# Conditioning vectors on VectorE, joined expert biases and gated rows, and a new seam between two blocks

## The chip, the cores and the metric

The kernel runs on one core of a Trainium2 chip, as one program. The metric is the time of one execution on the device in microseconds; the median of several runs counts. The core has TensorE (PE, with its weight loads listed as PEld), VectorE (DVE), ScalarE (ACT), GpSimd (POOL) and SyncE (SP), which here issues nearly all transfers from HBM.

## What is computed

256 tokens of 1024 channels pass through two blocks. Cut to what the change touches:

```python
def first_block(x, c, ctx, ...):
    mod_lat = split(silu(c) @ w_mod + b_mod, 6)        # 6 conditioning vectors of 1024
    h = rmsnorm(x, g) * (1 + mod_lat[1]) + mod_lat[0]
    x = x + mod_lat[2] * token_mixer(h, ...)           # latent attention + gated linear scan, w_in 1024x8256
    h = rmsnorm(x, g2) * (1 + mod_lat[4]) + mod_lat[3]
    x = x + mod_lat[5] * moe_ffn(h, ...)               # 32 experts, 4 per token
    return rmsnorm(x, final_norm_g)

def expert(xb, e):                                     # 1024 -> 2 x 1024 -> 1024
    gu = xb @ w_gate_up[e] + b_gate_up[e]
    act = swiglu(gu)
    return act @ w_down[e] + b_down[e]                 # weighted by the router, summed per token

def second_block(x, c_2, ...):
    mod = silu(c_2) @ w_ada + b_ada                    # 6 vectors of 1024
    h = modulate(rmsnorm(x, g_mix), sh1, sc1)
    ...                                                # recurrent mixer, then 32 small experts
    shf, scf = split(silu(c_2) @ w_ada_f + b_ada_f, 2) # 2 vectors, for the last norm
```

All is fp32. The weights make up nearly all of the 643 MB that are read.

## The kernel before

The program is recorded by a tile framework that places waits and orders each engine's instructions. Work comes in items of a queue: an `Item` has a part that asks for weights (`prep`) and a part that computes (`run`). `step()` prepares the first two items of the queue and runs the first; `fill(us)`, `need(item)` and `drain()` step through it, so that chains of other work (scan, attention) are interleaved with projections.

`wload` (L311) loads a weight tile of 128x2048 (1 MB) on SP's queue into the next of five slots; in MoE1 there are nine more (`w2x`, `w2`), 14 in all. A load whose slot is still read waits on SP, and every later load waits behind it. Projections (`tproj`) take a tile and split it into a high and a low part, a cast on ScalarE (L495) and a subtraction on VectorE (L496), both 128x1024, two for a tile of 1 MB; `mm3` (L508 to L510) makes three matmuls of 128x256 of each product, so a tile with eight row blocks is 48 matmuls.

**Block 1** (to 565 us) computes projections, the scan in four chains (0 to 3) and attention. Between the projections stand the "mods": one of 24 parts of 512 columns of a conditioning vector. `mod` loads two tiles of `wmod` or `wada`, and `modrow` makes 16 matmuls (L367) whose stationary operand holds the condition vector in one of 32 columns; VectorE adds the result into `rowall` (L369), one row per part. `fold_rows` and `mod_cols` turn the rows into columns when the block ends. 8 + 12 parts stand in block 1 (4 more for the first norm ahead of it), and the 4 of `wadaf` in block 2.

**MoE1** (577 to 1535 us) takes the 32 experts in turn, each of eight tiles `wgu` and four `wdn`, 12 MB. The rows of four experts, 64 each, are gathered at a time (L1278 to L1282). `expert1a` makes 64 matmuls gu (L1327) of 64 columns of tokens, in pairs for the two column halves, then the bias: four matmuls recorded, with a one-hot column as stationary operand against the table `brows` (L1402). `expert1b` transposes the activation, makes the 32 matmuls y (L1358), two of bias, and calls `combine`: yhi on ScalarE (L1236), ylo on VectorE (L1237), eight matmuls that scatter rows back to tokens (`co`, L1248), and per 128x512 piece of x a multiplication with the gate (L1253) and an addition (L1254) on VectorE. After expert 11 (`OVF`) the program looks whether some expert has more than 64 rows (L1292).

**The seam.** After the last expert x is normalised twice: once as the output of block 1 and once as the input of block 2. `xh` = x*gf (L1672), sums of squares (L1673, L1674), reciprocal roots (L431, L432); GpSimd multiplies x by r1 (L1681), VectorE xh by r2 (L1682); eight pairs of transposes (L1710); the results are scaled and shifted by VectorE (L1714) and ScalarE (L1715), and GpSimd makes the low part (L1716). Then the first projections of block 2 (`tproj` of `win2`) run, interleaved with a loop over low-rank products (`lora`, L1750 to L1760).

Of the kernel before, what the change touches and what calls it, by code (L numbers as in the profile page):

```python
# [18 lines left out]
EPS = 1e-6  # L19
# [4 lines left out]
MODS1 = [(1, j) for j in range(4, 12)] + [(2, j) for j in range(12)]  # L24
# [7 lines left out]
def _cols(a):  # L32
# [23 lines left out]
def _khalf(w):  # L56

    t = w.shape[1] // 512
    return np.ascontiguousarray(w.reshape(2, 4, 128, t, 512).transpose(3, 0, 2, 1, 4)).reshape(2 * t, 128, 2048)
# [62 lines left out]
def layout(i):  # L122
# [12 lines left out]
    d['wmod'] = _khalf(i['w_mod'][0])  # L135
    d['wmix'] = _ktile(i['w_mod'][0][:, :2048])
    d['wada'] = _khalf(i['w_ada_2'][0])
    d['wadaf'] = _khalf(i['w_ada_f_2'])
    mix = i['b_mod'][0][:2048].reshape(2, 4, 256).transpose(1, 0, 2).reshape(-1)
    d['bmods'] = np.ascontiguousarray(np.concatenate([mix, i['b_mod'][0][2048:], i['b_ada_2'][0], i['b_ada_f_2'], mix]).reshape(32, 512))  # L140
# [36 lines left out]
class Item:  # L177

    def __init__(self, prep, run):
        self.prep, self.run = prep, run  # L180
        self.ready = self.done = False
        self.gen = self.then = None
# [57 lines left out]
class Ker:  # L240
    def __init__(self, tc, d, out, dbg=None, stop=None, start=1):
        self.tc, self.nc, self.d, self.out = tc, tc.nc, d, out
        self.dbg = dbg or {}
        self.stop, self.start = stop, start
# [5 lines left out]
    def run(self):  # L250
        with ExitStack() as es:
# [10 lines left out]
            if self.start <= 1:  # L262
                with tc.tile_pool(name="t1late", bufs=1, side="right") as pl, tc.tile_pool(name="t1", bufs=1) as p:
                    self.early = lambda n: p.tile([128, 512], F32, name=n, tag="u", bufs=NU)
                    self.consts()
                    route = self.block1(p, pl, xtile)
            else:
                self.early = lambda n: self.cp.tile([128, 512], F32, name=n)
                self.consts()
                self.x1 = xtile("x").rearrange("p a (b n) -> p (a b n)", b=1).rearrange("p (b n) -> p b n", b=2)  # L270
                self.nc.sync.dma_start(self.x1, self.d['xin'])
                self.add(*(self.mod(2, j) for j in range(12)))
                self.drain()
                self.mod_cols((12, 10, self.mcol2[:, 0:40]))
# [4 lines left out]
            if self.start > 1:  # L279
                self.load_gf()  # L280
            if self.start <= 1:
                with tc.tile_pool(name="moe1", bufs=1, side="right", reuse_waits="tile") as p, tc.tile_pool(name="w2", bufs=NW2, reuse_waits="tile") as wp2, tc.tile_pool(name="w2x", bufs=NW2X, reuse_waits="tile") as wp3:
                    self.wq = own * NWR + [(wp3, "w")] * NW2X + [(wp2, "w")] * NW2
                    self.moe1(p, route, (wp2, "w"), (wp3, "w"))
# [29 lines left out]
    def consts(self):  # L314
# [23 lines left out]
        self.cpad2 = cp.tile([128, 504], F32, name="cpad2").rearrange("p (k n) -> p k n", k=8)  # L338
        nc.gpsimd.memset(self.cpad2, 0.0)
        nc.gpsimd.tensor_copy(self.cpad2[:, :, 31], cs[:, 16:24])  # L340
# [6 lines left out]
        self.mcol2 = cp.tile([128, 48], F32, name="mcol2")  # L347

# [4 lines left out]
    def msrc(self, which, j):  # L353
        src, r = {1: ('wmod', j), 2: ('wada', 12 + j), 3: ('wadaf', 24 + j)}[which]
        return [self.d[src][2 * j + a] for a in range(2)], r
# [15 lines left out]
    def mod(self, which, j):  # L371

        src, r = self.msrc(which, j)
        cpad = self.cpad1 if which == 1 else self.cpad2

        def run(ws):
            yield from self.modrow(cpad, r, [(0, lambda k: ws[k // 4][:, 512 * (k % 4):512 * (k % 4) + 512])])
        return Item(lambda: [self.wload(t) for t in src], run)
# [34 lines left out]
    def mod_cols(self, *todo):  # L413

        pt = self.fold_rows()
        for r, n, dst in todo:
            self.nc.vector.tensor_copy(dst.rearrange("p (j g) -> p g j", g=4), pt.rearrange("p (g r) -> p g r", g=4)[:, :, r:r + n])

    def bcast_rows(self, keys, dst, last=None):

        nc = self.nc
        for key, o in zip(keys, dst):
            ps = self.ps("bc")
            r = self.msrc(*key)[1]
            nc.tensor.matmul(ps, self.fold[:, r:r + 1].to_broadcast([128, 128]), self.rowall, start=True, stop=True)  # L425
            (last or nc.scalar.copy)(o, ps)
# [8 lines left out]
    def add(self, *items):  # L435
        self.q += items
        return items[-1]
# [99 lines left out]
    def block1(self, p, late, xtile):  # L537
# [255 lines left out]

        mods = [self.mod(*m) for m in MODS1]
        def mixed(items):
            out = []
            for it in items:
                out.append(it)
                if mods:
                    out.append(mods.pop(0))  # L800
# [66 lines left out]
        for pr in range(4):  # L867
# [4 lines left out]
            else:  # L872
                nxt = None
                lnexp()
                for i in range(3):
                    self.later(4 * i, lambda i=i: readout(i))
                self.add(*(tproj(win[28 + a], LAT, keep(qa, "qa", 3, qnorm)) for a in range(3)),
                         tproj(win[31], HS, keep(ckv, "ckv", 2, cnorm)), tproj(d['wrope'], HS, keep(kr, "kr"), nb=1, n=1024))
# [1352 lines left out]
```

## Time and profile before

| | us |
|---|---|
| median of 3 runs | 2112.69 (2109.07 to 2114.51) |
| the profiled execution, its own time | 2111.07 |
| its span in the trace | 2109.3 |

| engine | busy us | share of the span |
|---|---|---|
| PE | 1945.5 | 92% |
| PEld | 1114.6 | 53% |
| DVE | 896.0 | 42% |
| ACT | 511.6 | 24% |
| POOL | 63.3 | 3% |

The queue of weights (q1) takes 74.9% of the span of the 16 DMA engines; the mean rate is 306 GB/s. These shares are averages over stages with different limits, so the tables of windows, waits and single instructions are read stage by stage. Times in a timeline count from the span's start; a group of matmuls is listed with its start, its length and its count, and square brackets hold the idle time of the engine ahead of it and what ended that.

### The profile page before, as it was taken

The page shows a single profiled execution, that of the slowest core. Times are in us where ns is not written, and L with a number is a line of the kernel's source. Part 1 is how long each engine was busy: PE and PEld are TensorE (multiplying, and loading weights), DVE is VectorE, ACT ScalarE, POOL GpSimd, SP SyncE. Part 2 cuts the span into 40 slices and gives each one's busy share as a digit, 9 for nine tenths or more (in the row PEclk, how much of TensorE's full clock was granted, in tenths as well). Part 3 has the DMA queues.
Part 4 walks back from the last instruction along what each step waited for, and adds up shares of the span by engine and source line. Part 5 has one row for each costly group of instructions (what it writes and reads, how often), then busy time and mean ns, then how long its engine had stood idle before and what let it go on. Part 6 is the DMA issues. An engine that isn't in the chain of part 4 may idle for free. (4 is left out here: it accounts for less than half of the span.)

```text
span 2109.3 us, 30791 instructions
## 1 busy us (share of the span) xinstructions
PE 1945.5 (92%) x12860; PEld 1114.6 (53%) x12861; DVE 896.0 (42%) x1727; ACT 511.6 (24%) x893; POOL 63.3 (3%) x66
## 2 busy tenths in 40 slices
PE   5999999999899999989999999999969998899785
PEld 3888788877733333333333333333338997764331
DVE  5666754445423233332323333242378574421112
ACT  3433454344300001000000100000035543311011
POOL 0000000000000000000000000000032201000000
PEclk9999999999999999989999999999989999989897
DMA  9255636732699999979999999999873133289895
GB/s 362 81 219 201 227 126 258 278 111 80 262 415 427 411 427 416 427 295 407 426 427 427 426 427 427 426 427 427 365 292 124 62 121 103 114 370 420 360 425 226
DMA packets 95272, 646.11 MB, mean 306 GB/s; under 512 B 11668, under 2 KB 12692, under 8 KB 19220
## 3 DMA queue, kind: packets, MB, share of 16 engines
q1 hardware_dynamic: 93296, 642.79, 74.9%
q8 instruction: 104, 1.70, 0.3%
q10 hardware_dynamic: 1828, 1.26, 0.2%
q14 instruction: 44, 0.36, 0.0%
HBM read 642.96 MB, written 1.05 MB: 305 GB/s over the span
## 5 line engine op out<-in xcount | busy, mean ns | idle before, releaser
L1327 PE MATMUL gu<-w,gT 128*64 128x512 f32 x2048 | 481.2, 597 | 0.0
L1327 PEld LDWEIGHTS gu<-w,gT 128*64 128x64 f32 x2048 | 148.1, 137 | 278.1 <-issue 263.1
L1358 PE MATMUL y<-w,aT 128*64 128x512 f32 x1024 | 229.4, 601 | 0.4
L496 DVE TENSOR_TENSOR wsl<-w,wsh 128x1024 fp32r<-128x1024 f32 (+1 forms) x141 | 168.6, 1205 | 97.6 <-ACT wsh L495 97.3
L495 ACT CAST wsh<-w 128x1024 fp32r<-128x1024 f32 (+1 forms) x141 | 143.4, 1030 | 169.0 <-PE tp L509 97.4
L1337 DVE TENSOR_SCALAR act<-gu 128x256 f32<-128x256 f32 x64 | 27.2, 425 | 307.5 <-PE gu L1402 304.2
L1237 DVE SCALAR_TENSOR_TENSOR ylo<-y,sw,yhi 128x512 fp32r<-128x512 f32 x52 | 39.0, 751 | 264.5 <-ACT yhi L1236 264.0
L1358 PEld LDWEIGHTS y<-w,aT 128*64 128x64 f32 x1024 | 71.9, 139 | 148.6 <-issue 143.7
L508 PE MATMUL tp<-hs,wsh 128*128 128x256 f32 (+1 forms) x424 | 139.7, 329 | 0.0
L510 PE MATMUL tp<-hs,wsl 128*128 128x256 f32 (+1 forms) x424 | 134.3, 317 | 4.1 <-DVE wsl L496 4.1
L509 PE MATMUL tp<-hs,wsh 128*128 128x256 f32 (+1 forms) x424 | 133.6, 315 | 0.0
L1529 PE MATMUL ab<-w,gT 128*32 128x256 f32 (+1 forms) x1024 | 99.8, 415 | 17.4 <-DMA w<-in_w1e_dram 10.8
L1236 ACT ACTIVATE yhi<-y,sw 128x512 fp32r<-128x512 f32 x52 | 35.8, 688 | 300.9 <-PE y L1402 239.9
L1253 DVE TENSOR_TENSOR gated<-co,gtb 128x512 f32<-128x512 f32 x128 | 88.3, 690 | 34.6 <-PE co L1248 27.5
L1339 ACT ACTIVATE sge<-act 128x512 f32<-128x512 f32 x32 | 20.1, 630 | 331.3 <-DVE act L1337 331.3
L508 PEld LDWEIGHTS tp<-hs,wsh 128*128 128x128 f32 x424 | 81.7, 193 | 16.3 <-issue 4.9
L1254 DVE TENSOR_TENSOR x<-x,gated 128x512 f32<-128x512 f32 x128 | 88.3, 690 | 3.3
L510 PEld LDWEIGHTS tp<-hs,wsl 128*128 128x128 f32 x424 | 81.6, 193 | 9.9 <-DVE wsl L496 4.9
L508 PE MATMUL tp<-hi,wsh 128*128 128x256 f32 x288 | 85.4, 296 | 0.0
L509 PEld LDWEIGHTS tp<-hs,wsh 128*128 128x128 f32 x424 | 81.8, 193 | 4.5 <-issue 0.7
L1278 PE MATMUL ga<-oh,xhi 128*128 128x256 f32 x208 | 63.5, 333 | 21.9 <-PEq L1292 6.3
L509 PE MATMUL tp<-lo,wsh 128*128 128x256 f32 x288 | 81.7, 284 | 0.0
(576 smaller groups left out, 3099.9 us busy)
## 6 DMA issues: line engine op xcount, KB each, us to landing
w<-in_wgu_dram SPq DMA_DIRECT2D x256, 1024.0 KB, 15.3
w<-in_wdn_dram SPq DMA_DIRECT2D x128, 1024.0 KB, 15.6
w<-in_win_dram SPq DMA_DIRECT2D x50, 1024.0 KB, 5.9
w<-in_w3e_dram SPq DMA_DIRECT2D x32, 1024.0 KB, 14.7
w<-in_w1e_dram SPq DMA_DIRECT2D x32, 1024.0 KB, 11.9
w<-in_w2e_dram SPq DMA_DIRECT2D x32, 1024.0 KB, 15.9
w<-in_wada_dram SPq DMA_DIRECT2D x24, 1024.0 KB, 6.4
w<-in_wmod_dram SPq DMA_DIRECT2D x16, 1024.0 KB, 6.0
```

The costliest lines, as they stand in the source:

```text
L495: nc.scalar.copy(hi, src)
L496: nc.vector.tensor_sub(lo, src, hi.bitcast(F32))
L508: nc.tensor.matmul(out, a[0], b[0], start=first, stop=False)
L509: nc.tensor.matmul(out, a[0], b[1], start=False, stop=False)
L510: nc.tensor.matmul(out, a[1], b[0], start=False, stop=last)
L1237: nc.vector.scalar_tensor_tensor(lo, y, w, hi.bitcast(F32), op0=OP.mult, op1=OP.subtract)
L1253: nc.vector.tensor_mul(part, o[s], gate[:, cs])
L1254: nc.vector.tensor_add(x[:, b, cs], x[:, b, cs], part)
L1278: nc.tensor.matmul(ps[:, 256 * kk:256 * kk + 64 * n], xs[i][:, b, 128 * (k + kk):128 * (k + kk) + 128], ohv[b], start=(b + i == 0), stop=( ...
L1327: nc.tensor.matmul(gu[j][64 * s:64 * s + 64, :], g[:, k, c0:c0 + 64], w[:, 1024 * s + 512 * j:1024 * s + 512 * j + 512], start=(k == 0), s ...
L1358: nc.tensor.matmul(y[64 * s:64 * s + 64, :], aT[:, k % 4, k // 4, :], w[:, o:o + 512], start=(k == 0), stop=False)
L1529: nc.tensor.matmul(ps[m * j:m * j + m, 256 * i:256 * i + 256], g[:, k, c0 + m * j:c0 + m * j + m], w[j][:, k, :], start=(k == 0), stop=(k ...
```

## The change

It has four parts.

1. *Conditioning.* `w_mod`, `w_ada` and `w_ada_f` are stored by output column. A part of 512 columns is two "light" items of one tile each: VectorE multiplies 128x1024 weights with the condition vector, broadcast over partitions (`crow`: eight small matmuls and two copies, once for each of two vectors), and accumulates the sum into one column of `mcol` (L386 of the new kernel), twice, then adds the bias (L389). All 24 parts, the four of `wadaf` too, are 48 items of block 1: one behind each projection of the chains, two behind each g7 and wqb item. `step()` looks past light items until it has prepared two others.
2. *Joined biases.* In MoE1 the bias of gu is two matmuls and that of y one, each of 128 columns by 512, over both halves at once: the stationary operand is a block-diagonal one-hot (`brow`, 128x128, made by VectorE per expert), the other a table of high and low bias parts, loaded by 12 small DMAs and split once.
3. *Gated rows.* y is multiplied by the gate before it is split and combined (L1376), one 128x512 step per expert; `combine` only adds.
4. *Seam.* The down weights of expert 31 go into the nine MoE1 slots, and four tiles of `win2` are asked for behind them. xh is not scaled: the transposes become matmuls against diag(r2), into four PSUM tiles. x times r1 moves to ScalarE, behind the evacuations. The squares stand in a row with one reciprocal root.

```diff
+            def run(w):
+                yield 0
...
+                for i in range(2):
+                    wi = w[:, 1024 * i:1024 * i + 1024]
+                    n = 2 * a + i
+                    nc.vector.scalar_tensor_tensor(wi, wi, 1.0, c, op0=OP.mult, op1=OP.mult, accum_out=o[:, n:n + 1])
+                o = o[:, 2 * a:2 * a + 2]
+                b = VOFF[bias] + 4 * j + 2 * a
+                nc.vector.tensor_add(o, o, self.vec[:, b:b + 2])
+            return Item(lambda: self.wload(self.d[src][2 * j + a]), run, True)
+        return [half(0), half(1)]
...
     def step(self):
         it = self.q[0]
-        for i in self.q[:2]:
+        n = 0
+        for i in self.q:
             if not i.ready:
                 i.ready, i.w = True, i.prep()
+            n += not i.light
+            if n == 2:
+                break
...
-        lastg = [self.add(tproj(win[24 + i], LAT, g7)) for i in range(4)][-1]
+        lastg = [self.add(*mixed([tproj(win[24 + i], LAT, g7)], 2)) for i in range(4)][-1]
...
-            for s in range(2):
-                bias(gu[j][64 * s:64 * s + 64, :], 0, 1024 * s + 512 * j)
+            bias(gu[j], 0, 512 * j)
...
-        for s in range(2):
-            bias(y[64 * s:64 * s + 64, :], 1, 512 * s)
-        self.combine(p, x, y, oT, wv, gate)
+        bias(y, 1, 0)
+        part = p.tile([128, 512], F32, name="gated", tag="gated", bufs=1)
+        nc.vector.tensor_mul(part, y, gate)
+        self.combine(p, x, part, oT, wv)
...
+                return first.pop((e, j)) if (e, j) in first else fetch(e, j, ahead if e == 31 and j >= 8 else None)
...
+            rows = p.tile([128, 128], F32R, name="brow", tag="brow", bufs=2)
+            nc.vector.tensor_scalar(rows, blk, one, None, op0=OP.mult)
...
-        mods = [self.mod(3, j) for j in range(4)]
-        self.add(*mods)
-        for m in mods[:2]:
-            m.ready, m.w = True, m.prep()
-        ahead = [(self.wload(win2[2]),)]
+        ahead = {j: (self.wload(win2[j]),) for j in (2, 3, 0, 1)}
...
-            nc.gpsimd.tensor_mul(x[:, b, :], xh[b], r1[:, b:b + 1].to_broadcast([128, 1024]))
-            nc.vector.tensor_scalar(xh[b], xh[b], r2[:, b:b + 1], None, op0=OP.mult)
+            scaled = nc.vector.tensor_scalar(dg[:, 128 * b:128 * b + 128], self.ident, r2[:, b:b + 1], None, op0=OP.mult)
...
-                nc.tensor.transpose(pt[:, 128 * b:128 * b + 128], xh[b][:, 128 * k:128 * k + 128], self.ident)
+                nc.tensor.matmul(pt[k][:, 128 * b:128 * b + 128], xh[b][:, 128 * k:128 * k + 128], dg[:, 128 * b:128 * b + 128],
+                                 start=True, stop=True)
...
+        with tc.issue_after(evac.ins):
+            r1 = self.sm.tile([128, 2], F32, name="r1")
+            self.rstd_from(r1, st, 1024, self.eps)
+            for b in range(2):
+                nc.scalar.activation(x[:, b, :], xh[b], AF.Identity, scale=r1[:, b:b + 1])
```

VectorE in block 1, at the g7 items behind chain 3 (`wsl` is the low part of a projection's weights, `s` the scan's output). Before:

```order
L369 TENSOR_TENSOR rowall<-rowall,modps 128x512
L496 TENSOR_TENSOR wsl<-w,wsh 128x1024 x2
L864 TENSOR_TENSOR sg<-sg,tp 128x512
L865 TENSOR_TENSOR s_3680<-s_3680,sg 128x512
L369 TENSOR_TENSOR rowall<-rowall,modps 128x512
L496 TENSOR_TENSOR wsl<-w,wsh 128x1024 x9
L496 TENSOR_TENSOR wsl<-w,wsh 128x512
L496 TENSOR_TENSOR wsl<-w,wsh 128x1024
```

After:

```order
L878 TENSOR_TENSOR s_3575<-s_3575,sg 128x512
L507 TENSOR_TENSOR wsl<-w,wsh 128x1024 x2
L386 SCALAR_TENSOR_TENSOR w,mcol_97<-w,crow 128x1024 x2
L389 TENSOR_TENSOR mcol_97<-mcol_97,vec 128x2
L386 SCALAR_TENSOR_TENSOR w,mcol_97<-w,crow 128x1024 x2
L389 TENSOR_TENSOR mcol_97<-mcol_97,vec 128x2
L507 TENSOR_TENSOR wsl<-w,wsh 128x1024 x2
L386 SCALAR_TENSOR_TENSOR w,mcol_97<-w,crow 128x1024 x2
L389 TENSOR_TENSOR mcol_97<-mcol_97,vec 128x2
```

Between two projections' weight splits, where nothing or one addition stood, now stand four multiplications of 128x1024 and two additions.

PE in MoE1, one expert with the first gate/up matmuls of the next (`aT` transposes the activation, `wT` the router weights). Before:

```order
L1262 MATMUL wT<-fc,oh 64x128 x4
L1327 MATMUL gu<-w,gT 64x512 x24
L1402 MATMUL gu<-brows,fc 64x512 x4
L1358 MATMUL y<-w,aT 64x512 x16
L1402 MATMUL y<-brows,fc 64x512 x2
L1327 MATMUL gu<-w,gT 64x512
L1248 MATMUL co<-yhi,oT 128x512 x2
L1248 MATMUL co<-ylo,oT 128x512 x2
```

After:

```order
L1278 MATMUL wT<-fc,oh 64x128 x4
L1343 MATMUL gu<-w,gT 64x512 x24
L1447 MATMUL gu<-bra,brow 128x512 x2
L1373 MATMUL y<-w,aT 64x512 x16
L1447 MATMUL y<-brb,brow 128x512
L1343 MATMUL gu<-w,gT 64x512
L1262 MATMUL co<-yhi,oT 128x512 x2
L1262 MATMUL co<-ylo,oT 128x512 x2
```

The order is the same; the biases (L1402 before, L1447 after) are two instructions and one instead of four and two, at full width.

PE at the seam, from the last bias of expert 31 on. Before:

```order
L1402 MATMUL y<-brows,fc 64x512 x2
L1248 MATMUL co<-yhi,oT 128x512 x3
L1248 MATMUL co<-ylo,oT 128x512 x2
L1248 MATMUL co<-yhi,oT 128x512
L1248 MATMUL co<-ylo,oT 128x512 x2
L367 MATMUL modps<-w,cpad_91 32x512 x16
L1710 MATMUL xT<-fc,xh_11007 128x128 x3
L1710 MATMUL xT<-fc,xh_11008 128x128 x3
L1710 MATMUL xT<-fc,xh_11007 128x128
```

After:

```order
L1447 MATMUL y<-brb,brow 128x512
L1262 MATMUL co<-yhi,oT 128x512 x4
L1262 MATMUL co<-ylo,oT 128x512 x4
L1747 MATMUL xT<-dg,xh_10758 128x128 x8
L1747 MATMUL xT<-dg,xh_10759 128x128 x8
L519 MATMUL tp<-hi,wsh 128x256
L1805 MATMUL pw<-xm,lora_10781 64x256
```

The 16 matmuls of the first two late mods, which stood between the combination and the transposes, are gone, the transposes stand in two runs by row block, and the first projection follows them.

## Rows read from the trace of the kernel before

**Rows 1.** Windows, block 1; busy us of each engine, granted clock, DMA share, GB/s.
```profile
100.00:283.00 183.00, 183.00 (x1243) 148.74 (x1243) 115.77 (x280) 77.91 (x167) 0.00 (x0) 1.00 0.54 204
283.00:500.00 217.00, 212.02 (x1466) 173.35 (x1465) 112.62 (x192) 98.87 (x166) 0.00 (x0) 1.00 0.51 185
```

**Rows 2.** Waits of PE, 100 to 565 us: total, times, longest.
```profile
PE tp L510 <- DVE wsl L496: 4.1, 3, 1.6
```

**Rows 3.** Windows, the matmuls of the mods (L367) alone.
```profile
100.00:283.00 183.00, 23.91 (x192) 4.60 (x192) 1.00 0.54 204
283.00:500.00 217.00, 15.39 (x128) 3.34 (x128) 1.00 0.51 185
```

**Rows 4.** Groups of VectorE: busy us, mean ns, idle before.
```profile
L496 DVE TENSOR_TENSOR wsl<-w,wsh 128x1024 fp32r<-128x1024 f32 x135 | 164.4, 1228 | 91.5 <-ACT wsh L495 91.2
L369 DVE TENSOR_TENSOR rowall<-rowall,modps 128x512 f32<-128x512 f32 x28 | 19.1, 683 | 26.4 <-PE modps L367 26.2
L496 DVE TENSOR_TENSOR wsl<-w,wsh 128x512 fp32r<-128x512 f32 x6 | 4.1, 692 | 6.1 <-ACT wsh L495 6.1
L1138 DVE SCALAR_TENSOR_TENSOR xlo<-x,rs,xhi 128x1024 fp32r<-128x1024 f32 x4 | 4.9, 1278 | 0.0
```

**Rows 5.** Windows, MoE1.
```profile
578.00:878.00 300.00, 293.01 (x1472) 106.30 (x1468) 94.99 (x168) 25.07 (x40) 0.00 (x0) 0.99 1.00 418
904.00:916.00 12.00, 11.45 (x52) 3.15 (x48) 2.90 (x6) 1.07 (x2) 0.00 (x0) 1.00 0.08 30
938.00:943.00 5.00, 3.32 (x15) 3.35 (x16) 1.51 (x3) 0.56 (x1) 0.00 (x0) 0.50 0.22 57
984.00:1480.00 496.00, 481.86 (x2398) 171.64 (x2396) 167.77 (x292) 40.73 (x66) 0.00 (x0) 1.00 1.01 427
1517.00:1535.50 18.50, 16.86 (x72) 6.05 (x68) 6.62 (x10) 1.27 (x2) 0.11 (x1) 0.82 0.69 255
```

**Rows 6.** Timeline of ScalarE, the activation of an expert, four experts apart.
```profile
1100.38 0.63 ACT L1339 ACTIVATE sge<-act 128x512 f32<-128x512 f32 x1 [12.64 <-DVE act L1337]
...
1219.34 0.63 ACT L1339 ACTIVATE sge<-act 128x512 f32<-128x512 f32 x1 [12.64 <-DVE act L1337]
```

**Rows 7.** Timeline, one expert of MoE1.
```profile
1216.84 1.93 PE L1402 MATMUL gu<-brows,fc 32*64 32x512 f32 x8
...
1218.70 7.09 PE L1358 MATMUL y<-w,aT 128*64 128x512 f32 x32
...
1225.72 1.07 PE L1402 MATMUL y<-brows,fc 32*64 32x512 f32 x4
...
1228.90 0.69 DVE L1253 TENSOR_TENSOR gated<-co,gtb 128x512 f32<-128x512 f32 x1 [0.59 <-PE co L1248]
...
1232.84 0.42 PEld L1348 LDWEIGHTS aT<-fc,act 128*128 128x128 f32 x4 [0.81 <-DVE gated L1253]
```

**Rows 8.** Timeline, from the last expert to the first projection of block 2.
```profile
1534.47 1.07 PE L1402 MATMUL y<-brows,fc 32*64 32x512 f32 x4
...
1543.28 0.69 DVE L1254 TENSOR_TENSOR x<-x,gated 128x512 f32<-128x512 f32 x1
...
1546.38 0.16 DVE L1676 SCALAR_TENSOR_TENSOR tn<-tn,tn 128x1 f32<-128x1 f32 x1
...
1551.57 4.49 POOL L1681 TENSOR_TENSOR x<-xh,r 128x1024 f32<-128x1024 f32 x2 [18.56 <-ACT r L432]
...
1556.76 0.87 PE L1710 MATMUL xT<-fc,xh 128*128 128x128 f32 x3 [14.71 <-DVE xh L1682]
...
1568.57 0.47 PE L508 MATMUL tp<-hi,wsh 128*128 128x256 f32 x1
...
1569.11 0.28 PE L508 MATMUL tp<-hi,wsh 128*128 128x256 f32 x1
...
1570.41 0.28 PE L510 MATMUL tp<-hi,wsl 128*128 128x256 f32 x1
```

**Rows 9.** Waits of ScalarE, 1536 to 1570 us.
```profile
ACT wsh L495 <- DMA w<-in_win_dram: 5.1, 1, 5.1
```

More of the change, by code (lines that the diff above doesn't have):

```diff
@@ L261, in run @@
             self.last_sig = None
[L262 to L268, printed above, removed]
-                self.consts()
[L270 to L274, printed above, removed]
+            with tc.tile_pool(name="t1late", bufs=1, side="right") as pl, tc.tile_pool(name="t1", bufs=1) as p:
+                self.early = lambda n: p.tile([128, 512], F32, name=n, tag="u", bufs=NU)
+                self.consts()
+                route = self.block1(p, pl, xtile)
             if self.stop == 1:
@@ L369, in modrow, with crow, mod, half @@
         nc.vector.tensor_add(self.rowall, self.rowall, ps)
[L371 to L378, printed above, removed]
+    def crow(self, p, i):
+        nc = self.nc
+        t = p.tile([128, 1024], F32, name="crow", tag="crow")
+        for h in range(2):
+            ps = self.ps("cr")
+            for k in range(4):
+                o = 8 * i + 4 * h + k
+                nc.tensor.matmul(ps[:, 128 * k:128 * k + 128], self.cs[:, o:o + 1].to_broadcast([128, 128]), self.ident, start=True, stop=True)
+            nc.scalar.copy(t[:, 512 * h:512 * h + 512], ps)
+        return t
+    def mod(self, p, which, j):
+        nc = self.nc
+        src, bias = {1: ('wmod', 'b_mod'), 2: ('wada', 'b_ada_2'), 3: ('wadaf', 'b_ada_f_2')}[which]
+        def half(a):
+            def run(w):
+                yield 0
+                key = 0 if which == 1 else 2
+                if self.crows[0] != key:
+                    self.crows = key, self.crow(p, key)
+                c = self.crows[1]
+                o = self.mcol(which, j)
+                for i in range(2):
[7 more added lines that the diff above has]
+        return [half(0), half(1)]
     def mod_first(self, q, tile):
@@ L792, in block1, with mixed @@
                 s.forget(i, b, pf[i][b])
-        mods = [self.mod(*m) for m in MODS1]
-        def mixed(items):
+        self.crows = None, None
+        mods = [h for m in MODS for h in self.mod(p, *m)]
+        def mixed(items, n=1):
             out = []
@@ L1251, in combine @@
                 cs = slice(512 * s, 512 * s + 512)
[L1252 to L1253 removed]
+                part = o[s]
+                if gate is not None:
+                    part = p.tile([128, 512], F32, name="gated", tag="gated", bufs=1)
+                    nc.vector.tensor_mul(part, o[s], gate[:, cs])
                 nc.vector.tensor_add(x[:, b, cs], x[:, b, cs], part)
@@ L1741, in done @@
                 return f
-            return [self.tproj(ahead[0] if i == 1 and j == 0 else win2[2 * i + j], HS, done(j)) for j in range(2)]
+            return [self.tproj(ahead.pop(2 * i + j, win2[2 * i + j]), HS, done(j)) for j in range(2)]
         ik, ir, iv = shifted(1), shifted(0), shifted(2)
         self.add(*ik, *ir, *iv)
+        for i, last in enumerate((scaled, evac)):
+            with tc.issue_after(last.ins):
+                ik[i].ready, ik[i].w = True, ik[i].prep()
         pw, pg = self.pg("pw"), self.pg("pg")
```

148 lines of the change are left out of this document (78 added, 70 removed), and 3 rows, old and new, of the table VECS.

## The prediction

> **What bounds the kernel now.** I read three stretches by the windows view, then inside each the waits and the timeline. In block 1 (100 to 500 us) the columns to look at are PE busy, DVE busy and DMA share: PE is busy 183.00 of 183 us and 212.02 of 217, DVE 115.77 and 112.62, DMA share 0.54 and 0.51 [rows 1]. PE's list of waits between 100 and 565 us holds 4.1 us for weight splits as its largest line [rows 2]. So TensorE is the bound there, and VectorE has some 40% of its time free. In MoE1 (578 to 1535 us) PE is busy nearly throughout too, but the DMA share is 1.00 to 1.01 at 418 to 427 GB/s over the same windows [rows 5]. Two limits lie on top of each other: the activation of the first of four experts comes again after 1219.34 - 1100.38 = 118.96 us [rows 6], and 48 tiles of 1 MB (1.0486 MB at 427 GB/s is 2.456 us) take 117.9 us. PE is the slower by 1 us in 119, and whatever PE is relieved of beyond that is met by the transfers. In the seam between MoE1 and block 2 there is one chain through VectorE, ScalarE and GpSimd, with PE waiting for most of it [rows 8].
>
> **Conditioning (block 1).** Removed: 20 mods of 16 matmuls on PE, 23.91 us between 100 and 283 (12 mods) and 15.39 us between 283 and 500 (8) [rows 3], of time in which PE has no other gap. VectorE loses the adds into rowall, 0.683 us each [rows 4], 8.2 and 5.5 us. Added: 48 halves on VectorE, each two scalar_tensor_tensor of 128x1024 with an accumulated sum and a small add. No row of before has that operation with an accumulator. The nearest is the scalar_tensor_tensor 128x1024 of split_tokens, 1.278 us, with two fp32 operands in SBUF, beside the subtraction of the same size at 1.228 [rows 4]. I take 1.28, since only the sum differs; with the small add, 0.16 us by the row of a one-column scalar_tensor_tensor [rows 8], a half is 2 x 1.28 + 0.16 = 2.7 us and 48 are 130 us. Bounds for the instruction: 1.23, and twice the row, 2.56.
>
> The Trainium skill, in "Vector Engine (DVE) Microarchitecture Reference", section 7 (Points that are easy to get wrong), says that this family with two SBUF sources that are not bf16 runs at half throughput. The row of 1.278 us has two such sources and takes what the plain subtraction takes, so the trace disagrees for the form without a sum; for the form with one, which no row shows, the halving is the rival D below.
>
> VectorE's load then is, from 100 to 283 us, 115.8 - 8.2 + 16 x 2.7 = 150.8 us, against 159 us of PE work left; from 283 to 500 it is 112.6 - 5.5 + 32 x 2.7 = 193.5 us against 212 - 15.4 = 196.6. The order shows 16 halves before chain 3 and 32 behind it. In the first stage VectorE has a little room, and in-order waiting costs part of it: I take 20 of the 24 us as gain (the eight broadcast matmuls of `crow` and its copies come off it too). In the second stage the halves bunch. A g7 projection (48 matmuls; eleven steps from 1569.11 to 1570.41 [rows 8] are 0.118 us each, so 5.7 us) comes with two halves, so VectorE owes 2 x 1.23 for splits + 2 x 2.7 = 7.9 us per item; a wqb item has 36 matmuls, 4.3 us, against 1.23 + 0.69 [rows 4] + 5.4 = 7.3. Four and six such items are 75 us of VectorE against 49 us of PE, 26 us too much. Half of that I expect to be filled by scan readouts, kv items and the attention that follows; the rest, plus waits for an in-order queue, eats the 15.4 us and about 5 more. Here the DMA issues of the halves matter as well: three 1 MB tiles per g7 item are 7.4 us of transfer, in five slots, no worse than VectorE. Block 1: 20 - 5 = **15 us** gained; bounds -10 (VectorE sets both stages) and 30 (both covered).
>
> **Joined biases and gated rows (MoE1).** Before, eight half-wide matmuls for gate/up last from 1216.84 to 1218.70, 1.86 us, and four for down from 1225.72 to 1226.72, 1.00 us [rows 7]. They become two and one of 128x512. Their price is not in the trace; the nearest are 32 half-wide ones in 7.09 us, 0.22 each [rows 7]. So 1.86 + 1.00 - 3 x 0.22 = 2.2 us less per expert (at 0.5 each, if a full-width one costs what two half-wide ones do and more, 1.36). The gate on y puts one DVE step of 0.69 us [rows 7] ahead of the yhi/ylo/combine chain, for which PE already waits; I charge it whole, 0.7. Dropping four multiplications behind the combination frees the PSUM that the transposes wait 0.81 us for [rows 7]: about 0.4 us back. PE gains 2.2 - 0.7 + 0.4 = 1.9 us per expert, bounds 0.7 and 2.3; the one-hot rows, 128x128 on VectorE once per expert, lie in ScalarE's yhi step. The bias loads (12 small DMAs on SP, behind the first gate/up tiles and ahead of gf) go out while slots are full; the three copies and six subtractions once are at most some 4 us, at the first expert, and PE recovers it in two.
>
> 32 x 1.9 = 61 us of PE work is not 61 us of time: four experts become 119.0 - 7.6 = 111.4 us, under the transfers' 117.9. So I count by the transfers. At 578 us, where PE takes up the first expert, all 14 slots have been asked for and filled, and 370 tiles are to come; 370 x 2.456 = 909 us, plus 6 us because the first 300 us ran at 418 GB/s [rows 5], give a last landing near 1493; the 1517 of before is 24 us later, 15 of them the idle stretch below and the rest the 1.06 us per four experts, some 5 us, and small gaps. The sum assumes that the loader no longer stands idle at the overflow look after expert 11, where shares of 0.08 and 0.22 over 12 and 5 us add up to 11.0 + 3.9 = 15 us [rows 5]: by then PE has gained 12 x 1.6 = 19 us on the loader, so about eight slots are empty when PE stops, 20 us of cover. And PE's lag behind the last landing (1517 to 1535.5, 18.5 us [rows 5, 8]) shrinks to the last tile's work, 4 us, and some 3 us for an imperfect cover. The end of expert 31's y moves from 1535.5 to about 1500: **35 us**, bounds 20 (PE gains only 1.2 us per expert and keeps half of both stalls) and 42.
>
> **The seam.** Reckoned from the end of the last y bias, 1535.54 us. The combination alternates eight DVE steps of 0.69, of which the last starts at 1543.28 [rows 8]; five remain, 2 us less. From the GpSimd multiplication at 1551.57 to the first transpose at 1556.76 are 5.2 us [rows 8]; two 128x128 diagonals take their place, each at most the 0.69 of a 128x512 step [rows 4]; at 0.4 each that is 4.4 us less. The four squares in a row with one rstd save 1 to 2 us. The two late mods leave PE, and ScalarE's 5.1 us wait for the first win tile [rows 9] goes, since four of them are asked for straight behind the last down weights. Until the first projection that is 2 + 4.4 + 1.5 + 5 to 8 = 13 to 16 us of the 33.0 between 1535.54 and 1568.57. But the projections share PE with the lora loop, which GpSimd feeds (the lo subtractions and shifted differences start no earlier than the evacuations), and x times r1 now stands on ScalarE behind them. I let 1 to 4 us be lost to that: **11 us**, bounds 6 and 16. Behind the seam nothing is changed.
>
> **Sum.** 2111.07 - 15 - 35 - 11 = 2050 for the profiled execution, which is 1.6 us under the median of the runs; against the median, 2052 us.
>
> **Rivals.** A: VectorE becomes the bound of block 1. For it: 75 against 49 us in the g7 and wqb items; against it: the sums over the stages still fit. Price: block 1 from +15 to -8, 2075 us.
> B: MoE1 was the transfers' all along, and the two stalls stay because slots refill before expert 11 and at the end. For it: 427 GB/s before as after; against it: PE's margin grows with every expert. Only 10 of 35 us arrive: 2077 us.
> C: everything is covered: 30 + 42 + 15 = 87 us, 2026 us.
> D, slower than before: the multiplication with an accumulated sum takes twice the row, 2.56 us. VectorE then owes 150.8 + 41 = 192 us and 193.5 + 82 = 275 us in the two stages, 467 in all, where 400 us passed before. Block 1 is 67 us longer, the other parts give 46 back: 2111 + 67 - 46 + 1.6 = 2134. It decides from a loss of 46 us on, which is VectorE at 446 us, or (446 - 344) / 96 = 1.06 us more per instruction, 2.34 us. The trace of before neither shows nor excludes it; 1.278 us without the sum speaks against.
> That the change does not move what it says I leave out, since the order shows halves, joined biases and early tiles at their new places.
>
> **How the numbers follow.** Forecast 56% (2040 to 2064), A 20%, B 12%, C 6%, D 4%, a mixture of A and B that ends within 0.3% (6 us, about what a measurement of this kernel can tell from no change) 2%. The range runs over the forecast, A and B and to the edge of C: 2030 to 2084. Faster by over 0.3%: 0.94; within: 0.02; slower: 0.04.
>
> **What would show it.** The DVE row of the new conditioning line at about 1.28 us, x96; PE's waits in block 1 naming weight splits by 10 to 25 us, between the g7 and wqb items (under 5: C; over 40: A). In MoE1, 48 tiles every 118 us, PE with short waits for tiles instead of SP waiting for PE; no window of DMA share under 0.5 after expert 11; y of expert 31 ending within 7 us of the last landing. At the seam, the first projection 17 to 20 us after the last bias. The prediction is wrong if TensorE's clock falls in MoE1 when it starts to wait (granted 1.00 in the steady window, but 0.50 between 938 and 943 us, where it had paused [rows 5]) and PE becomes the bound again, or if GpSimd decides the seam.

## The result, and the profile after

The changed kernel takes 2056.01 us (median of 4 runs, 2054.82 to 2057.85) against 2112.83 us for the kernel before (median of 4 runs): a ratio of 0.9734, 95% interval 0.9717 to 0.9751. The forecast of 2052 us was 4 us low, and the range held it.

The sum came out, its terms did not. From landmarks that both traces hold (start of the first gate/up matmul, end of expert 31's y bias, last instruction):

| stretch | before, us | after, us | gained | forecast |
|---|---|---|---|---|
| block 1, to the first gate/up matmul | 576.0 | 545.8 | 30.2 | 15 |
| MoE1, to the end of the last y bias | 959.5 | 945.0 | 14.5 | 35 |
| seam and all behind it | 568.4 | 558.8 | 9.6 | 11 |
| sum | | | 54.3 | 61 |

The spans of the two traces differ by 55.6 us and the medians by 56.8; the 1.3 us between the table's sum and the spans lie behind the last computing instruction.

The page of the changed kernel, its first part (busy time, share of the span, instructions):

```profile
span 2053.7 us, 29758 instructions
...
PE 1851.9 (90%) x12300; PEld 1119.0 (54%) x12301; DVE 925.7 (45%) x1885; ACT 517.1 (25%) x899; POOL 56.7 (3%) x62
```

Block 1 in windows, as [rows 1], with 50 us out of the g7 and wqb items besides:

```profile
100.00:283.00 183.00, 182.98 (x1233) 167.69 (x1232) 159.41 (x383) 92.44 (x195) 0.00 (x0) 1.00 0.50 176
283.00:500.00 217.00, 207.25 (x1344) 172.80 (x1343) 177.94 (x348) 97.66 (x167) 0.00 (x0) 0.97 0.69 255
350.00:400.00 50.00, 41.68 (x300) 38.59 (x298) 42.17 (x72) 16.68 (x22) 0.00 (x0) 0.93 0.86 328
```

VectorE went from 115.77 to 159.41 us and from 112.62 to 177.94. Until 283 us PE shows no gap, as forecast; between 350 and 400 it is idle for 8.3 us and its granted clock is 0.93, with VectorE at 42 of 50 us and transfers at 0.86. The new operation's group, beside [rows 4] (busy us, mean ns of one, idle before):

```profile
L386 DVE SCALAR_TENSOR_TENSOR w<-w,crow 128x1024 f32<-128x1024 f32 x96 | 115.5, 1223 | 1.3 <-DMA w<-in_wmod_dram 1.3
...
L386 DVE DVE_READ_ACCUMULATOR w<-w,crow 128x1 f32 x96 | 8.4, 87 | 0.0
...
L389 DVE TENSOR_TENSOR mcol<-mcol,vec 128x2 f32<-128x2 f32 x48 | 7.7, 160 | 0.5
```

A multiplication with an accumulated sum takes 1.223 us, and each is followed by a separate read of the accumulator, 0.087 us. A half costs 2 x 1.31 + 0.16 = 2.78 us, against the 2.7 of the forecast. PE's waits in block 1, as [rows 2] (total us, times, longest):

```profile
PE tp L519 <- ACT wsh L506: 6.3, 3, 3.0
PE kn L519 <- ACT wsh L506: 1.6, 1, 1.6
PE kn L521 <- DVE wsl L507: 0.9, 1, 0.9
PE tp L521 <- DVE wsl L507: 0.8, 1, 0.8
```

MoE1 in windows, as [rows 5]; the second is the overflow look after expert 11:

```profile
600.00:850.00 250.00, 236.91 (x1166) 91.12 (x1163) 71.41 (x139) 21.29 (x34) 0.00 (x0) 0.99 1.01 419
890.00:905.00 15.00, 12.08 (x57) 6.69 (x57) 2.11 (x5) 1.70 (x3) 0.00 (x0) 0.77 0.71 287
950.00:1450.00 500.00, 458.98 (x2234) 172.82 (x2232) 133.19 (x260) 41.23 (x66) 0.00 (x0) 0.99 1.01 419
```

The transfers are never idle for long now: 0.71 over 15 us at the look, 4 us lost, where [rows 5] had 15 (only from 898 to 902 us the share is under 0.5, at 0.28). But the rate is 419 GB/s where [rows 5] has 427 in the steady window. The waits of SP, which issues the loads, for 600 to 1450 us:

```profile
SPq L300 <- DMA w<-in_wgu_dram: 411.5, 198, 4.6
SPq L300 <- DMA w<-in_wdn_dram: 204.9, 97, 9.6
SPq L300 <- PE gu L1343: 56.5, 43, 5.4
SPq L300 <- PE y L1373: 23.4, 18, 4.4
```

Before, PE headed the same list:

```profile
SPq L311 <- PE gu L1327: 334.6, 173, 14.2
SPq L311 <- PE y L1358: 156.4, 75, 17.8
```

Now the loader waits for its own earlier transfers, and PE for tiles, among others: its own list for these 850 us has 23.1 us for `yhi` and, next,

```profile
PE y L1373 <- DMA w<-in_wdn_dram: 13.2, 26, 0.6
```

That the transfers and not the chain through `yhi` set the pace is shown by their share of 1.01 and by the run with the old gate below. Four experts apart, as [rows 6], the pair of activations that [rows 6] showed 118.96 us apart:

```profile
1171.18 0.63 ACT L1354 ACTIVATE sge<-act 128x512 f32<-128x512 f32 x1 [13.62 <-DVE act L1352]
...
1291.05 0.63 ACT L1354 ACTIVATE sge<-act 128x512 f32<-128x512 f32 x1 [13.62 <-DVE act L1352]
```

119.87 us. Yet early in MoE1, while the slots are still full, the same distance is 565.01 to 677.60:

```profile
565.01 0.63 ACT L1354 ACTIVATE sge<-act 128x512 f32<-128x512 f32 x1
...
677.60 0.63 ACT L1354 ACTIVATE sge<-act 128x512 f32<-128x512 f32 x1 [8.95 <-DVE act L1352]
```

112.6 us is the pace of PE alone; the forecast had 111.4. The first four experts of the kernel before take 120.1 us:

```profile
595.14 0.63 ACT L1339 ACTIVATE sge<-act 128x512 f32<-128x512 f32 x1 [7.48 <-DVE act L1337]
...
715.21 0.63 ACT L1339 ACTIVATE sge<-act 128x512 f32<-128x512 f32 x1 [9.74 <-DVE act L1337]
```

So PE was relieved as reckoned, by 7.5 us per four experts, and the transfers took over, at a pace that was slower than reckoned.

The seam, as [rows 8]:

```profile
1490.30 0.50 PE L1447 MATMUL y<-brb,brow 128*128 128x512 f32 x1
...
1501.18 5.35 PE L1747 MATMUL xT<-dg,xh 128*128 128x128 f32 x32 [7.26 <-DVE dg L1719]
...
1507.78 0.39 PE L519 MATMUL tp<-hi,wsh 128*128 128x256 f32 x1 [1.25 <-ACT hi L1754]
```

The transposes start 10.4 us after the end of the bias (1490.80) instead of 21.2, the first projection 17.0 us after it instead of 33.0.

### The profile page after: what moved, and what is told of

Same layout as the page of the kernel before. It is cut to its first block, busy times and chain, and to the rows that moved or that the text cites. A ratio compares the mean times of both kernels' runs of the same rounds, so it can differ in the third digit from the quotient of the medians.

```text
span 2053.7 us, 29758 instructions
## 1 busy us (share of the span) xinstructions
PE 1851.9 (90%) x12300; PEld 1119.0 (54%) x12301; DVE 925.7 (45%) x1885; ACT 517.1 (25%) x899; POOL 56.7 (3%) x62
## 5 line engine op out<-in xcount | busy, mean ns | idle before, releaser
L1343 PEld LDWEIGHTS gu<-w,gT 128*64 128x64 f32 x2048 | 157.3, 137 | 259.7 <-issue 230.7
L1373 PE MATMUL y<-w,aT 128*64 128x512 f32 x1024 | 233.9, 599 | 15.7 <-DMA w<-in_wdn_dram 14.8
L386 DVE SCALAR_TENSOR_TENSOR w<-w,crow 128x1024 f32<-128x1024 f32 x96 | 115.5, 1223 | 1.3 <-DMA w<-in_wmod_dram 1.3
L1376 DVE TENSOR_TENSOR gated<-y,gtb 128x512 f32<-128x512 f32 x32 | 22.1, 692 | 183.1 <-PE y L1447 183.1
L1270 DVE TENSOR_TENSOR x<-x,co 128x512 f32<-128x512 f32 x128 | 79.4, 683 | 18.8 <-PE co L1262 18.8
L1250 ACT ACTIVATE yhi<-gated,sw 128x512 fp32r<-128x512 f32 x32 | 23.1, 721 | 249.9 <-DVE gated L1376 249.9
```

What stands on the lines that cost most here:

```text
L386: nc.vector.scalar_tensor_tensor(wi, wi, 1.0, c, op0=OP.mult, op1=OP.mult, accum_out=o[:, n:n + 1])
L1270: nc.vector.tensor_add(x[:, b, cs], x[:, b, cs], part)
L1343: nc.tensor.matmul(gu[j][64 * s:64 * s + 64, :], g[:, k, c0:c0 + 64], w[:, 1024 * s + 512 * j:1024 * s + 512 * j + 512], start=(k == 0), s ...
L1373: nc.tensor.matmul(y[64 * s:64 * s + 64, :], aT[:, k % 4, k // 4, :], w[:, o:o + 512], start=(k == 0), stop=False)
```

## Experiments

Each run below is compared with runs of the kernel before on the same chip (their medians lie between 2108.7 and 2112.8 us, so medians of different groups of runs can differ by 4 us for nothing); where medians are set against 2056.01 us, the ratios to before stand beside them, and that of the changed kernel is 0.9734 (0.9717 to 0.9751). The interval between landings is the median over consecutive 1 MB tiles of MoE1, from the trace's record of issues and landings: 2.443 us in the trace of before, 2.492 in that of the changed kernel.

**Does the rate belong to the program?** Both kernels were run again, unchanged, on one chip.

> The kernel before once more, for its rate of transfers in MoE1 beside the changed kernel's. If the 2.49 us from one 1 MB tile's landing to the next that the changed kernel shows (2.44 in the first trace of before) belongs to the execution, this run shows a value of either kind, the same as the changed kernel's run beside it. If it belongs to the program, this run shows 2.44 and the other 2.49.

> The changed kernel once more. By the program: 2.49 us per tile again, 945 us from the first gate/up matmul to the end of expert 31's bias. By the execution: the same interval as the run of before beside it; at 2.44 the stretch would be 384 x 0.05 = 19 us shorter, or less where TensorE then is the later.

Measured: 2115.57 us and 2053.68 us, intervals 2.44 and 2.492 us. The rate belongs to the program: two executions of each agree, on one chip. It does not hang on how many tiles are under way either: within the changed kernel the interval is 2.49 with three under way and with seven.

**Gated rows** undone: the gate again in the combination.

```diff
-        nc.vector.tensor_mul(part, y, gate)
-        self.combine(p, x, part, oT, wv)
+        self.combine(p, x, y, oT, wv, gate)
```

> The changed kernel with the gate back in the combination: four multiplications of 128x512 more per expert on VectorE behind the combining matmuls, one step less ahead of them. Theory (transfers bound MoE1, PE has 6 us of 118 to spare per four experts): 0 to 2 us slower. Rival (TensorE still bounds MoE1): the step ahead goes, 0.7 us per expert, the wait of the transposes comes back, 0.8, so 0 to 5 us slower with PE waiting for VectorE and none of it for tiles.

Measured: 2058.86 us, ratio 0.9762 (0.9746 to 0.9779). MoE1 took 943.2 us, no longer than with the change (945.0), and PE alone, in the first four experts, 112.2 us against 112.6. What is lost, about 3 us, is at the seam: the first transpose comes 14.2 us after the last bias instead of 10.4, since four multiplications stand between the additions again. So this part is worth its steps in the tail of the last expert and nothing in the 31 before.

**Joined biases** undone: four and two half-wide fp32 matmuls, tables of 32 rows.

```diff
-            bias(gu[j], 0, 512 * j)
+            for s in range(2):
+                bias(gu[j][64 * s:64 * s + 64, :], 0, 1024 * s + 512 * j)
...
-        bias(y, 1, 0)
+        for s in range(2):
+            bias(y[64 * s:64 * s + 64, :], 1, 512 * s)
```

> The changed kernel with four and two half-wide bias matmuls in fp32 per expert again: 2.2 us of PE more per expert. Theory (transfers bound MoE1): four experts are 112 + 8.8 = 121 us of PE against 119.6 of transfers at 2.49 us per tile, so PE is the bound again by a little: 8 to 20 us slower, the stretch of MoE1 953 to 965 us. Rival (TensorE bounds MoE1 throughout): 32 x 2.2 = 70 us slower.

Measured: 2074.66 us, ratio 0.9835 (0.9818 to 0.9851): 18.7 us slower, MoE1 962.5 us, and PE alone 120.8 us for the first four experts. The theory's upper end; the 70 us of the rival are excluded. The windows show PE as the bound again at the same transfer rate:

```profile
950.00:1450.00 500.00, 486.29 (x2398) 176.23 (x2400) 132.97 (x244) 41.82 (x67) 0.00 (x0) 0.98 1.01 420
```

486.29 of 500 us busy, against 458.98 with joined biases.

**Where the slots stand.** The built programs place the 14 weight slots of MoE1 at multiples of 256 bytes in each partition of SBUF in the kernel before, and 32 bytes past such a multiple in the changed one, because its table of constant vectors grew and a padded condition vector went. Two runs move all tiles behind the first constant tile:

```diff
-        self.vec = cp.tile([128, NVEC], F32, name="vec")
+        self.vec = cp.tile([128, NVEC + 8], F32, name="vec")[:, :NVEC]
```

with 8 columns (32 bytes), after which the slots begin 64 bytes past a multiple of 256, and with 56 (224 bytes), after which they begin at one.

> The changed kernel with the first constant tile 32 bytes wider in each partition, nothing else: the 14 weight slots of MoE1 then begin at multiples of 64 bytes as in the kernel before, where the changed kernel's begin 32 bytes off them. Theory (the start of a slot sets the 2.49 us of a tile against 2.44): tiles land every 2.44 us again, MoE1 is 384 x 0.049 = 19 us shorter at most, 15 to 19 us, total 2037 to 2041. Rival (the rate comes from something else in the program, such as the layout in HBM or the order of issues): 2.49 again and no change, 2054 to 2058.

Measured: 2052.28 us, ratio 0.9718 (0.9700 to 0.9735), interval 2.484 us. The theory fell as I had put it: to begin at multiples of 64 bytes brought 0.008 of the 0.049 us, and a gain that the intervals don't separate from none. I formed it anew with a coarser grain:

> The changed kernel with the first constant tile 224 bytes wider in each partition, nothing else: the 14 weight slots of MoE1 then begin at multiples of 256 bytes, as those of the kernel before do; the 32-byte shift left them at odd multiples of 64. Theory (what counts is the slot's start at a coarser grain than 64 bytes): tiles land every 2.44 us, MoE1 15 to 19 us shorter, total 2037 to 2041. Rival (the place of the slots doesn't matter, and the 0.008 us of the first shift were chance): 2.48 to 2.49 again, 2051 to 2056.

Measured: 2039.65 us, ratio 0.9658 (0.9641 to 0.9674), interval 2.445 us; MoE1 took 931.6 us, 13.4 less than in the changed kernel and a little under the 15 to 19 of the theory; of the 16.4 us in all, 2.1 lie ahead of MoE1, where executions of the changed kernel differ by as much. The steady windows:

```profile
600.00:850.00 250.00, 236.86 (x1171) 91.89 (x1169) 71.83 (x140) 21.87 (x35) 0.00 (x0) 0.99 1.01 427
950.00:1450.00 500.00, 469.80 (x2300) 181.69 (x2296) 135.84 (x264) 41.96 (x67) 0.15 (x2) 0.99 1.01 427
```

427 GB/s again, and PE busy for 469.80 us of 500. The control moves the slots of the kernel before off their places by the same 8 columns:

> The kernel before with its first constant tile 32 bytes wider in each partition, nothing else, so that its slots begin where the changed kernel's do. Theory (place of the slots): tiles land every 2.49 us instead of 2.44; since transfers of 119.6 us then exceed the 119.0 of TensorE per four experts by a little, 0 to 8 us slower. Rival (place doesn't matter): 2.44 again and no change.

Measured: 2111.70 us, ratio 0.9999 (0.9990 to 1.0009), interval 2.492 us:

```profile
600.00:850.00 250.00, 243.15 (x1208) 88.26 (x1204) 81.44 (x143) 20.10 (x33) 0.00 (x0) 0.99 1.01 419
950.00:1450.00 500.00, 485.83 (x2450) 174.66 (x2448) 165.51 (x292) 41.12 (x67) 0.00 (x0) 1.00 1.01 418
```

418 GB/s where [rows 5] has 427, at no cost: in the kernel before PE is late by its own work, and the last landing moved from 1517.1 to 1526.5 us, into the 18.5 us for which PE lagged behind it. The same loss that costs the changed kernel some 16 us was free before it.

The padding moves every tile behind it, not the slots alone. That the slot counts is shown inside single executions, in MoE2. Its tiles go to the five common slots and to eight slots of its own, which the built program of the kernel before places 160 bytes past a multiple of 256. In the trace of before (intervals from 2.2 to 2.7 us) a tile for a common slot lands 2.436 us after the tile ahead of it (median of 22), a tile for one of the eight 2.487 us (42); with 224 bytes of padding, which leaves both kinds at these distances, it is 2.438 (16) and 2.486 (37). So the place of the slots sets the rate.

**Conditioning** on TensorE as before, all 24 parts in block 1 (the extra table is sized so that the slots stay where the changed kernel has them).

```diff
-        mods = [h for m in MODS for h in self.mod(p, *m)]
+        mods = [self.mod(*m) for m in MODS]
```

> The changed kernel with all 24 parts of conditioning computed on TensorE in block 1 as before (16 matmuls each, 1.9 us), nothing on VectorE but the row additions; the seam keeps no conditioning. Theory (VectorE covers most of the 48 halves): block 1 is 24 x 1.93 = 46 us longer by TensorE's work, less the 8 to 12 us in which it now waits for weight splits: 33 to 40 us, all of it in the total, 2089 to 2096. Rival A of the prediction (VectorE had become the bound of block 1): 5 to 15 us slower.

Measured: 2096.72 us, ratio 0.9929 (0.9912 to 0.9947): 40.7 us slower, and the first gate/up matmul comes 35.5 us later. VectorE covers most of the 48 halves. Rival A is out. (This is not the old kernel's block 1: it had 20 parts there, and the run has 24.)

**VectorE's price doubled.**

```diff
+                    nc.vector.tensor_tensor(wi, wi, wi, op=OP.max)
                     nc.vector.scalar_tensor_tensor(wi, wi, 1.0, c, op0=OP.mult, op1=OP.mult, accum_out=o[:, n:n + 1])
```

> The changed kernel with one more elementwise step of 128x1024 in place on VectorE ahead of each of the 96 multiplications (maximum of the weights with themselves, about 1.23 us), so that a half costs what rival D supposed. VectorE would then owe 337 + 118 = 455 us for the stretch of 100 to 500 us in which it has 337 busy. Theory of the prediction's sum (VectorE decides from there on): 50 to 70 us slower, 2106 to 2126, with PE waiting for weight splits. Rival (there is more room on VectorE than the windows show, because attention follows): 15 to 35 us slower.

Measured: 2111.93 us, ratio 1.0003 (0.9992 to 1.0014): 55.9 us slower, all of it before the first gate/up matmul (56.0 us later). VectorE is the bound:

```profile
100.00:300.00 200.00, 199.98 (x1341) 182.92 (x1340) 196.20 (x429) 102.94 (x216) 0.00 (x0) 1.00 0.46 163
300.00:400.00 100.00, 89.73 (x637) 85.10 (x636) 99.57 (x157) 40.41 (x66) 0.00 (x0) 0.93 0.65 230
400.00:500.00 100.00, 79.35 (x427) 61.28 (x426) 95.20 (x159) 33.21 (x57) 0.00 (x0) 0.88 0.62 215
```

Up to 300 us it still hides behind PE, at 196.20 of 200 us; from there PE is idle for 10 and 21 us. At 1.22 + 1.23 = 2.45 us per multiplication the whole change is worth nothing, near the 2.34 us at which rival D was to decide.

**The seam, its tiles.** Only one tile of block 2 asked for early, expert 31's down weights in the common rotation.

```diff
-        ahead = {j: (self.wload(win2[j]),) for j in (2, 3, 0, 1)}
+        ahead = {2: (self.wload(win2[2]),)}
```

> The changed kernel in which only one tile of block 2's first projections is asked for at the seam and expert 31's down weights stay in the common rotation of slots; the new scaling stays. Theory (the early tiles take away ScalarE's 5 us wait for a tile, and the projections then overlap the low-rank loop): the first projection 2 to 6 us later and the total 2 to 6 us slower. Rival (GpSimd and the low-rank loop decide the seam, not the tiles): 0 to 1 us.

Measured: 2056.26 us, ratio 0.9734 (0.9717 to 0.9751); the first projection comes 18.0 us after the last bias instead of 17.0, the rest of the kernel is as long to within 1.1 us. The rival holds: the early tiles bring nothing that can be measured once no conditioning weights stand ahead of block 2's tiles.

**The seam, its scaling.** GpSimd and VectorE scale as before, plain transposes, old order of the squares.

```diff
-            scaled = nc.vector.tensor_scalar(dg[:, 128 * b:128 * b + 128], self.ident, r2[:, b:b + 1], None, op0=OP.mult)
+            nc.gpsimd.tensor_mul(x[:, b, :], xh[b], r1[:, b:b + 1].to_broadcast([128, 1024]))
+            scaled = nc.vector.tensor_scalar(xh[b], xh[b], r2[:, b:b + 1], None, op0=OP.mult)
```

> The changed kernel with the old scaling at the seam: x times r1 on GpSimd, xh times r2 on VectorE, plain transposes, the squares in the old order; the four early tiles stay. Theory (this chain is what PE waits for): the transposes begin 4 to 7 us later, total 4 to 7 us slower. Rival (the low-rank loop and PE's projections decide the seam): 0 to 2 us.

Measured: 2060.93 us, ratio 0.9764 (0.9747 to 0.9780), 4.9 us slower. The transposes wait for the old chain (first row of PE's waits of this run, then of the changed kernel, both from 1485 to 1512 us):

```profile
PE xT L1748 <- DVE xh L1720: 12.6, 1, 12.6
```

```profile
PE xT L1747 <- DVE dg L1719: 7.3, 1, 7.3
```

12.6 - 7.3 = 5.3 us, the theory.

**A better version.** One light item instead of two behind each g7 and wqb projection, so that ten of the 48 halves run under attention, and all slots at multiples of 256 bytes, MoE2's too.

```diff
-        lastg = [self.add(*mixed([tproj(win[24 + i], LAT, g7)], 2)) for i in range(4)][-1]
+        lastg = [self.add(*mixed([tproj(win[24 + i], LAT, g7)])) for i in range(4)][-1]
...
-        off = p.tile([128, 97], F32, name="off")
+        off = p.tile([128, 128], F32, name="off")[:, :97]
```

> The changed kernel with all weight slots at multiples of 256 bytes (MoE1's as in the run before, MoE2's eight further ones too, by a wider tile of its own) and one light item instead of two behind each g7 and wqb projection, the ten left over behind the last keys and values, where attention follows. Theory (in the stretch of 350 to 400 us TensorE loses 8 us to VectorE's bunched halves, while VectorE is half idle during attention): 3 to 8 us less than with the slots alone, and 0 to 4 us in MoE2: 2028 to 2037. Rival (what is put off then holds slots that MoE1's first tiles need, and MoE1 is bound by transfers): 2038 to 2046.

Measured: 2022.05 us (5 runs, 2020.75 to 2027.56), ratio 0.9596 (0.9582 to 0.9610). That is 17.6 us less than with the slots alone, more than the 3 to 12 I expected. Block 1 ends 14.5 us earlier and what lies behind the last y bias is 3.4 us shorter. PE in the window that lost 8.3 us above:

```profile
350.00:400.00 50.00, 49.93 (x370) 45.19 (x369) 44.60 (x74) 24.58 (x34) 0.00 (x0) 1.00 0.94 343
400.00:450.00 50.00, 49.85 (x290) 35.80 (x290) 45.82 (x102) 21.26 (x43) 0.00 (x0) 1.00 0.79 278
```

49.93 of 50 us, at a granted clock of 1.00. In the run with the slots alone the same two windows read 42.52 and 48.60 us, with 0.90 in the first:

```profile
350.00:400.00 50.00, 42.52 (x295) 39.41 (x293) 42.13 (x75) 15.67 (x21) 0.00 (x0) 0.90 0.88 327
400.00:450.00 50.00, 48.60 (x273) 34.34 (x274) 45.64 (x98) 24.26 (x45) 0.00 (x0) 1.00 0.87 305
```

The idle 8.9 us are one part of the 14.5. Another is the clock, which was at the lower of its two levels (1.2 and 2.4 GHz) for a part of the first window, where PE had paused: from the end of the g7 items to the end of the wqb items PE is busy for 86.42 us with the slots alone, at a mean granted clock of 0.96, and for 81.87 us here, at 1.00, with the same 483 matmuls. 8.9 and 4.5 make 13 of the 14.5 us; no run holds the two apart. Nor does this run tell VectorE's time from the slots that its halves hold, since it relieves both.

## Why the prediction was right, and where it was not

*What bounds the kernel.* Right: TensorE in block 1, with VectorE idle enough to take the conditioning (40.7 us are lost when 24 parts of it go back to TensorE); TensorE and transfers on top of each other in MoE1 (18.7 us for the old biases, not 70).

*Conditioning, the price.* 1.28 us was taken for the multiplication, 1.223 + 0.087 measured, 2.78 us per half against 2.7. The half throughput that the Trainium skill states ("Vector Engine (DVE) Microarchitecture Reference", section 7) is not what the row shows: 1.223 us with two fp32 sources and the sum, beside 1.235 for the subtraction of the same size. Rival D supposed 2.56 us; with the price doubled by hand the kernel ends at 2111.9 us and not at 2134, block 1 at 601.8 us, 25.8 longer than before and not 67. Of 118 us more on VectorE only 56 became delay, where the sum by stages counted every microsecond over the old stage as lost.

*Conditioning, the sum.* This is the first term that was mis-sized, by 15 us. VectorE's load came nearly as reckoned, 337 us in the two stages against 344. Up to the end of the scan (the last `gram` matmul, 330.9 us before and 312.5 after) the gain is 18.4 us, close to the 20 of the forecast. The step that failed is "the rest, plus waits for an in-order queue, eats the 15.4 us and about 5 more": from there to the first gate/up matmul the kernel gains another 11.8 us. The g7 items lose nothing: their last matmul ends at 381.2 us instead of 420.4, 39 us earlier. The stretch of the wqb items behind them, with keys, values and a part of attention, gives back 12: it takes 94.8 us instead of 82.8 for the same 483 matmuls. Some 6 of these 12 are idle time (7.3 us against 0.9), and the rest the clock (granted 0.95 instead of 1.00, PE busy for 87.5 us instead of 81.9), for which the forecast had no term. So VectorE's excess of 26 us over PE in ten items was right in kind and too large as a delay: PE's list of waits shows 9.6 us. Nor is it VectorE's time alone. 7.9 of the 9.6 us are waits for casts on ScalarE, and during the longest, 3.0 us up to 384.21, VectorE stands idle for 4.2 us; the tile to be cast was asked for at 377.32 and landed at 382.11, and SP's waits for slots from 300 to 420 us all name VectorE. How much of the loss comes through held slots and how much through VectorE's queue stays open. The bunching was real all the same: taking it away gave the 14.5 us of the last run.

*Joined biases and gated rows, PE's time.* Right: 120.1 to 112.6 us for four experts, 7.5 against 7.6. Inside it the parts differ: the gated rows bring nothing to it (112.2 us with the old gate, where the forecast charged 0.3 us per expert), and the biases carry it (120.8 us with the old ones), though two full-width matmuls take 0.73 us and the single one 0.50, where 0.22 each was taken.

*Joined biases and gated rows, the transfers.* This is the second term, 20.5 us too high. The mechanism held: PE runs ahead of its tiles, the idle stretch at the overflow look shrinks from 15 to 4 us, PE ends 6.1 us after the last landing (1484.7) instead of 18.5. The step that failed is "370 x 2.456 = 909 us": the price of a tile was read from a row of before, and the change itself raised it to 2.50 (419 GB/s), by moving the slots. At the old places MoE1 is 27.9 us shorter than before, within the bounds of 20 to 42. The other 7 us to 35 lie in the transfers too: with the slots at multiples of 256 bytes the last tile lands 924.0 us after the first gate/up matmul, where the forecast has 1493 - 576 = 917, and PE ends 7.6 us behind it, where the forecast has 7. Some 5 of them are the overflow look, which the forecast put at nothing and where two tiles land 5.6 and 4.0 us after the one ahead; the rest is not traced to a cause.

*The seam.* 9.6 us against 11, by its own steps: the first projection 17.0 us after the last bias where 17 to 20 were named, 5.3 us from the diagonals and the new order of the squares, which one run undid together, where 4.4 + 1.5 were reckoned, about 3 from the gate where 2 were. The early tiles were no part of it, at 1 us or less. Of the 16 us gained at the first projection 7.2 are left when the last group of low-rank products begins (L1772 before, L1819 after). Up to there PE is busy for 30.15 of 30.96 us, and it has 30 matmuls of the projections more behind it than before at the same point, 3.5 us, so a part of the difference was only moved forward.

*Rivals.* A is out: block 1 gains 30.2 us where A has a loss of 8. In block 1 it was C that came, with its 30, and nowhere else. B was right that the transfers bound MoE1, wrong that the two stalls stay. D has its mechanism shown (VectorE can become the bound), its price refuted by 1.223 us and its time by 2111.9. TensorE's clock did not turn MoE1 round: 0.99 in its steady windows, where the kernel waits for tiles. The forecast of the sum was within 4 us by luck, because +15, -20 and -1 nearly cancel; it was not right in its parts.

## What to carry to other kernels

When a change relieves an engine in a stage where another limit lies just above it, the other limit sets the gain, and its price has to be taken from the changed program: here a table that grew by some columns moved the weight buffers and made every transfer 2% dearer, which cost nothing as long as TensorE was late and 16 us afterwards. Check where the destinations of large transfers begin whenever a tile ahead of them changes size. And before work is handed to a half-idle engine, look at how it is bunched: the sum over the stage fitted, and 14 us were still lost in the stretch in which it did not.

## What was not expected of the hardware

Transfers of 1 MB tiles of 128 x 8192 bytes land every 2.44 us when the slot begins at a multiple of 256 bytes in each partition, every 2.484 us at 64 bytes past one and every 2.492 us at 32 (427, 421 and 419 GB/s); 0 and 32 were seen in both kernels, and at 32 the interval is the same with three tiles under way as with seven. MoE2's own slots add three places: 160 bytes past a multiple of 256 in the kernel before (2.487 us), 192 in the changed one (2.484) and 224 in the run with 32 bytes of padding (2.492); moved to a multiple of 256, in the last run, they take 2.443. So every place seen but the multiple of 256 costs about 2%. 96 and 128 were not tried, and no run shows why. VectorE's accumulated sum is two instructions, 1.223 and 0.087 us.
